# A bidirectional state-space layer with a feed-forward block: where zeroing, states, sums and one unit's restore are placed

## The chip, the cores and the metric

The kernel runs on one core of a Trainium2 chip. The metric is the time of one launch on the device in microseconds, as the median of some executions; lower is better. Engines: PE multiplies matrices, DVE, ACT and POOL work on vectors, SP only issues transfers. All of them run their own queues in order and wait for each other by semaphores.

## The reference

One layer (DEPTH = 1) over 1024 latent tokens of width 1024 with 256 context tokens ahead of them: a bidirectional S5 mixer (64 groups of 16 channels, 64 complex states each), a GLU, and a SwiGLU block of hidden width 2816. All in fp32.

```python
def run(u, h0):                                   # one direction
    bu = jnp.einsum('lgh,gnh->lgn', u.astype(F32), b_bar)
    bu = bu.at[0].add(lam_bar * h0)
    a = jnp.broadcast_to(lam_bar, bu.shape)
    _, h = lax.associative_scan(_linear_combine, (a, bu), axis=0)
    return jnp.einsum('lgn,ghn->lgh', h, c_mat).real, h[-1]
...
y = y.reshape(h.shape).astype(h.dtype) + d_skip * h      # forward + backward
g = jax.nn.gelu(y)
return g * jax.nn.sigmoid(g @ w_glu + b_glu)
...
x = x + m_l[2][:, None] * y_l
h_l = modulate(rms_norm(x, norm_ffn[i]), m_l[3][:, None], m_l[4][:, None])
x = x + m_l[5][:, None] * swiglu(h_l, ffn_w1[i], ffn_w3[i], ffn_w2[i])
```

## The kernel before

Tokens are cut into chunks of T = 8: 32 context chunks and 128 latent ones. Per chunk and group the inputs are summed into one state contribution, the states are scanned over the chunks, and an output is the sum of two parts: a Toeplitz product of the chunk's own inputs (`x_mm`) and a product of the state at its edge with coefficients CL (`states_mm` for half of the chunks, `states_all` for all). Groups come in eight units of 8 groups (0 to 7), two units to a quarter q. A unit's outputs are four groups of columns in two PSUM tiles, one for each parity of the group.

The scan runs on DVE (`scan`): 32 steps over two chunks each for the first 64 latent chunks, then 63 single steps. The odd chunks it skips in the first half are restored afterwards: for quarters 0 and 2 within the scan, for 1 and 3 by POOL (`fill`, op F). Early half means the states that the first 64 chunks of the scan give, late half the rest; backward states are turned into a buffer of their own (`turned`: R early, Z late, z both).

What runs beside the scan is written out by hand in the string PROG1, what runs after it in PROG2; `run` emits the operations in that order, and each engine's queue takes its instructions in the order of emission. A letter is an operation, its number a unit (K, P, R, N, D, H, Z, Q, z), twice a unit plus a parity (Y), a quarter and a part (C), or a load (T):

- C: `cl_ops`, one part of CL: two products on POOL and their sum, by PE and ACT (P in HOWS), POOL (E) or an accumulating DMA that POOL issues (Y).
- K: `k_mats`, the kernel matrices of half a quarter: 64-row products on PE into two PSUM tiles that ACT has zeroed before (`zeros`), two ACT copies, two writes to DRAM (`kd`) that ACT issues. T: SP loads them back as Toeplitz blocks KQ. T8 to T11 need K4 and K5, T12 to T15 need K6 and K7.
- P: early half of a unit, `x_mm` and then `states_mm`, which needs R; Y: two ACT copies of its tiles to SBUF. N: late half, D: two DVE adds of it onto Y.
- Q: a whole unit, `x_mm` and `states_all` (units 6 and 7). H: GELU on ACT. I, J: transposes for the GLU and their high and low parts. g: first GLU products.
- M, m, A, L, G, B: modulation, its loads, coefficient loads and signs.

The tiles of K, P and C come from a ring of three PSUM buffers (`pw`) beside two fixed ones, and those of PROG2 from eight (`pe8`) over the same eight banks. Later, in the FFN, each weight tile is split into a high part (ACT) and a low part, the rest (POOL): `op_split`, L1243. Its first four splits are emitted after the seventh GLU unit of the second half, L1261.

Of the kernel before, what the change touches and what calls it, by code (L numbers as in the profile page):

```python
# [17 lines left out]
P = 128  # L18
# [5 lines left out]
T = 8  # L24
G = 64
HC = 16
NS = 64
EPS = 1e-6
MAGIC = 12582912.0
HOWS = "PPPP PPEE PEEE EEEE"  # L30
ZEN = "VVSVSVSV"
PROG1 = ("A22 B0 A26 C02 G1 A30 A34 C03 A40 K0 A44 A48 C10 K1 L2 A54 G2 C11 A60 F10 C12 F11 C13 T0 T1 T2 T3 A64 M0 M1 K2 R0 P0 Y0 Y1 K3 L3 R1 C20 P1 Y2 Y3 T4 T5 G3 T6 T7 C21 C22 C23 K4 R2 P2 Y4 Y5 K5 R3 P3 Y6 Y7 T8 T9 T10 T11 C30 C31 R4 P4 Y8 Y9 C32 C33 R5 P5 Y10 Y11 K7 K6 M2 m0 F30 F31")
PROG2 = ("T12 T13 T14 T15 Z0 N0 Z1 Z2 D0 Z3 N1 D1 Z4 H0 H1 N2 D2 H2 w0 w1 l1 N3 Z5 D3 H3 N4 D4 z6 z7 I0 J0 I1 J1 H4 N5 D5 I2 J2 H5 I3 J3 W0 W1 W2 W3 x0 x1 x2 x3"
         " Q6 H6 I4 J4 Q7 I5 J5 V1 b0 w20 w21 l1 H7 g03 g13 I6 J6 g23 g05 g15 I7 J7 V2 g26 x10 x11 x12 x13")
LOG2E = 1.4426950408889634
LN2H = 0.693359375
LN2L = -2.12194440e-4
# [5 lines left out]
def s5_ffn_kernel(tc, a, out):  # L43
# [3 lines left out]
    with ctx:  # L47
# [16 lines left out]
        R0 = region("r0", 7)  # L64
# [594 lines left out]
        def cl_ops(q, part, ct, how):  # L659
# [7 lines left out]
            def add():  # L667
# [8 lines left out]
                else:  # L676
# [14 lines left out]
                 7: [(1, [0], 0, 8)], 8: [(1, [0], 8, 16)], 9: [(1, [1, 2, 3])],  # L691
                 11: [(2, [0], 0, 8)], 12: [(2, [0], 8, 16)], 13: [(2, [1, 2, 3])],
                 14: [(3, range(4), 0, 8)]}
        ct_ = [view(r, kb, [8, T, HC]) for r, kb in ((RW, 0), (RC[3], 0), (RC[3], 4), (RA, STB))]
        cts = [[ct_[0], ct_[0], ct_[1], ct_[2]], [ct_[0], ct_[1], ct_[2], ct_[0]], [ct_[1], ct_[2], ct_[0], ct_[1]], [ct_[3], ct_[0]] * 2]
        CL0 = cl_ops(0, 0, cts[0][0], SY) + cl_ops(0, 1, cts[0][1], SY)
        CLAT = {12: 1, 13: 1, 14: 2}
        for hb in range(16):
# [164 lines left out]
            while rest:  # L863
                one()

        def fill(q, h, reg, kb):

            tmps = [view(reg, kb + i, [256]) for i in range(2)]
            st, c0 = STQ[q], 32 * h
            for e in (0, 8):  # L870
                rot(st[:, 32 + c0:63 + c0:2, :, e:e + 8], st[:, 31 + c0:62 + c0:2, :, e:e + 8], LS[:, 0], 16 * q + e, E, tmps)

        MBd = dr.tile([2, 2, 512], F32, tag="mbd", name="mbd")

# [34 lines left out]
        def yview(k, gp):  # L909
            return Y[:, k].rearrange("p t (a e h) -> p e a t h", e=2, h=HC)[:, gp]  # L910

        def states_mm(k, pts, half, hs, start):

            for a_ in range(4):
                for ri in range(2):
                    for d in range(2):
                        cs_ = slice(64 * (half ^ d), 64 * (half ^ d) + 64)
                        c0 = 31 + 64 * half
                        for gp in range(2):
                            ps = slice(64 * gp, 64 * gp + 64)  # L920
                            st = hs[ps, :, ri, a_] if d else STQ[k // 2][ps, c0:c0 + 64, ri, 8 * (k % 2) + a_]
                            PE.matmul(flat(pts[gp][cs_, a_]), st, flat(CL[k // 2][ps, ri, d, 4 * (k % 2) + a_]),
                                      start=start and ri == 0, stop=ri == 1 and (start or a_ == 3))

        def states_all(k, pts, hs):

# [10 lines left out]

        def x_mm(k, pool):

            pts = [pool([4, T, HC]) for _ in range(2)]  # L940
            for a_ in range(4):
                for gp in range(2):
                    g = 2 * a_ + gp
                    kq = KQ[(2 * k + g // 4) % 4][:, g % 4].rearrange("p (t h) -> p t h", t=T)[:, ::-1]
                    PE.matmul(pts[gp][:, a_], U[:, 8 * k + g, 32:160], kq, start=a_ == 0, stop=False)
            return pts

        scan()
        inner = {}
        HSe = [view(r, kb, [64, 2, 4]) for r, kb in ((RC[3], 14), (RC[3], 12), (RC[3], 14), (RC[3], 12), (RA, 2), (RA, 0))]  # L950
        HSl = [view(RA, STB * (i // 3) + 4.125 + 2 * (i % 3), [64, 2, 4]) for i in range(6)]
        HSq = {6: view(RA, 0, [P, 2, 4]), 7: view(RA, STB, [P, 2, 4])}

        def run(prog):


            for w in prog.split():
                op, i = w[0], int(w[1:])
                if op == "A":
                    ada(i)  # L960
                elif op == "M":
                    mod_cols(i)
                elif op == "K":
                    k_mats(*divmod(i, 2), [zeros(pw([15 * HC])) if i == 6 else kt, zeros(pw([15 * HC])) if i in (0, 1, 2, 3, 6) else pm[:, 0:15 * HC]])
                elif op == "L":
                    cs_load(i, S)
                elif op == "G":
# [4 lines left out]
                elif op == "C":  # L972
                    q, part = divmod(i, 10)
                    for f in cl_ops(q, part, cts[q][part], HOW[q][part]):
                        f()
                elif op == "F":
                    fill(*divmod(i, 10), *((RW, 0) if i >= 30 else (RC[3], 12)))
                elif op == "T":
                    toeplitz(i)
                elif op == "R":  # L980
                    turned(i, 0, HSe[i], S)
                elif op == "Z":
                    turned(i, 1, HSl[i], ENG[ZEN[i]])
                elif op == "z":
                    turned(i, 2, HSq[i], ENG[ZEN[i]])
                elif op == "P":
                    inner[i] = x_mm(i, pw)
                    states_mm(i, inner[i], 0, HSe[i], False)
                elif op == "Q":
                    inner[i] = x_mm(i, pe8)  # L990
                    states_all(i, inner[i], HSq[i])
                elif op == "Y":
                    S.copy(yview(i // 2, i % 2), inner[i // 2][i % 2])
                elif op == "N":
                    late[i] = [pe8([4, T, HC]) for _ in range(2)]
                    states_mm(i, late[i], 1, HSl[i], True)
                elif op == "D":
                    for gp, po in enumerate(late[i]):
                        tt(yview(i, gp), po, yview(i, gp), ADD)
                elif op == "H":  # L1000
                    if i in late:
                        S.activation(Y[:, i], Y[:, i], AF.Gelu_apprx_tanh)
                    else:
                        for gp in range(2):
                            S.activation(yview(i, gp), inner[i][gp], AF.Gelu_apprx_tanh)
                elif op == "I":
                    if GH[0] is None:
                        GH[0] = tuple(view(region(t, 16, R32), 0, [4, 8, P]) for t in ("c1", "c0"))
                    late[i] = gt_hi(i, 0)
                elif op == "J":  # L1010
                    gt_lo(i, 0, late[i])
                elif op == "W":
                    if not W0:
                        W0.append(region("c2", 16, R32))
                        late["wh"] = view(W0[0], 0, [8, 512])
                    V.tensor_copy(view(W0[0], 4 * i, [1024]), wr0[i])
                elif op == "w":
                    cq, h = divmod(i, 10)
                    SY.dma_start(wr0[h], a["w_glu"][cq // 2][:, 1024 * h:1024 * h + 1024])
                elif op == "b":  # L1020
                    SY.dma_start(bglu, a["b_glu"].to_broadcast([P, D]))
                elif op == "l":
                    load_glu()
                elif op == "m":
                    mod_row(0)
                elif op == "x":
                    gate(i % 10, slice(4 * (i // 10), 4 * (i // 10) + 4))
                elif op == "V" and i == 2:
                    for j in range(4):
                        v = slice(1024 * j, 1024 * j + 1024)  # L1030
                        split(wr0[j], (WR[1][0][:, v], WR[1][1][:, v]), E)
                elif op == "V":
                    GR.append(region("ra", 80.5, R32))
                    GH[1] = (view(GR[0], 16, [4, 8, P]), view(GR[0], 32, [4, 8, P]))
                    WR.append((view(W0[0], 0, [8 * 512]), view(GR[0], 0, [8 * 512])))
                    WR.append((view(GR[0], 48, [8 * 512]), view(GR[0], 64, [8 * 512])))
                    for j in range(4):
                        v = slice(1024 * j, 1024 * j + 1024)
                        tt(WR[0][1][:, v], wr0[j], WR[0][0][:, v].bitcast(F32), SUB, (E, V)[j // 2])
                elif op == "g":  # L1040
                    glu_h(i // 10, i % 10 + 1)
# [198 lines left out]
            S.copy(o[0], x)  # L1240
            tt(o[1], x, o[0].bitcast(F32), SUB, eng)

        def op_split(ft, j, x):  # L1243
            o = ring[(4 * min(ft, NPL) + 7 * max(ft - NPL, 0) + j) % 4]
            OP_[ft, j] = o
            t_split([t.rearrange("p k n -> p (k n)") for t in o], x, E)

        RMS = {0: (0, 4), 4: (4, 6), 6: (6, 7)}
        for u in range(8):
# [8 lines left out]
            glu_unit(cq, s, *gens)  # L1258
            if u == 6:
                for j in range(4):  # L1260
                    op_split(0, j, raw[:, j])  # L1261
                raw13(1)
        together(rms_steps(7, 8))
        psE.__exit__(None, None, None)
# [520 lines left out]
```

## Time and profile before

| | us |
|---|---|
| median of three executions | 1013.72 (1013.44 to 1017.66) |
| profiled execution, whole | 1015.75 |
| profiled execution, span | 1014.0 |
| PE busy | 956.7 (94% of the span) |
| DVE, ACT, POOL busy | 781.7, 431.0, 761.1 |
| mean granted clock of PE | 0.991 |

The span runs from the first instruction to the last; the difference to the whole is what lies around it. Times in the rows below count from the span's start. Busy time of an engine doesn't say what bounds it: the tables of stretches and the waits do. The change lies between 195 and 260 us (end of PROG1, start of PROG2) and near 360 us (start of the FFN).

### The profile page before, as it was taken

Reading aid. Unit: us, or ns where it says so; the run is one execution under the profiler, and the core shown is the slowest. Engines: PE = TensorE matmul, PEld = TensorE weight load, DVE = VectorE, ACT = ScalarE, POOL = GpSimd, SP = SyncE. Lnnn points to the kernel's source line nnn. Section 1 sums busy time; section 2 is a strip of 40 time slices with the busy share of each in tenths; the row PEclk is TensorE's granted clock in tenths of the full one; section 3 lists DMA queues with packets and bytes.
Section 4 is the critical chain, followed back from the end, with each engine's and each line's share of the span. In section 5 each row is a group of like instructions: output and inputs, shape, how many; then the busy total and the mean of one; then the engine's idle time right before and its main releaser. Section 6 shows DMA issues by size and latency. Waiting matters only on the chain. (4 is left out here: it accounts for less than half of the span.)

```text
span 1014.0 us, 17677 instructions
## 1 busy us (share of the span) xinstructions
PE 956.7 (94%) x6604; PEld 751.5 (74%) x6604; DVE 781.7 (77%) x1594; ACT 431.0 (43%) x812; POOL 761.1 (75%) x590
## 2 busy tenths in 40 slices
PE   5988798879999999999999999999999999999996
PEld 1466523678888878778888888888888888888885
DVE  7979699996366767877959677686959677686887
ACT  5487622225444563443343343324343343324337
POOL 5799999994553448979785878777786877777764
PEclk9999999989999999999999999999999999999999
DMA  9765997325521021011212111121212111111205
GB/s 335 281 137 95 277 358 238 94 75 147 185 87 42 1 104 63 24 44 49 73 42 83 42 53 42 48 67 53 73 42 83 43 50 45 49 66 53 73 22 166
DMA packets 48542, 98.90 MB, mean 98 GB/s; under 512 B 4284, under 2 KB 18876, under 8 KB 47176
## 3 DMA queue, kind: packets, MB, share of 16 engines
q1 hardware_dynamic: 43272, 86.64, 25.8%
q0 software_dynamic: 2016, 7.34, 3.8%
q10 hardware_dynamic: 3168, 3.79, 1.1%
q8 instruction: 52, 0.85, 0.4%
q14 instruction: 34, 0.28, 0.1%
HBM read 84.25 MB, written 6.17 MB: 89 GB/s over the span
## 5 line engine op out<-in xcount | busy, mean ns | idle before, releaser
L77 POOL TENSOR_TENSOR c<-rxc,c 128x512 fp32r<-128x512 f32 x128 | 166.6, 1315 | 52.4 <-ACT c L1240 51.5
L1299 PE MATMUL ut<-ra,c 128*128 128x512 f32 x400 | 155.8, 389 | 1.2 <-DVE ra L77 1.2
L1298 PE MATMUL ut<-ra,c 128*128 128x512 f32 x400 | 155.8, 390 | 0.2 <-ACT ra L1240 0.2
L1300 PE MATMUL ut<-ra,c 128*128 128x512 f32 x400 | 155.7, 389 | 0.0
L1240 ACT CAST c<-rxc 128x512 fp32r<-128x512 f32 x128 | 79.0, 622 | 147.6 <-PE xt L1593 53.0
L1593 PE MATMUL xt<-c,c 128*128 128x512 f32 x540 | 129.7, 389 | 0.0
L1593 PEld LDWEIGHTS xt<-c,c 128*128 128x128 f32 x540 | 101.4, 188 | 21.0
L77 DVE TENSOR_TENSOR ru<-ru,xt 128x1024 f32<-128x1024 f32 x90 | 107.2, 1214 | 10.1 <-PE xt L1593 7.5
L77 DVE TENSOR_TENSOR ru<-ut,ru 128x512 f32<-128x512 f32 x98 | 67.1, 686 | 43.7 <-PE ut L1300 38.3
L1299 PEld LDWEIGHTS ut<-ra,c 128*128 128x128 f32 x400 | 75.1, 188 | 17.0 <-POOL rxc L77 1.5
L1298 PEld LDWEIGHTS ut<-ra,c 128*128 128x128 f32 x400 | 75.1, 188 | 16.1 <-ACT ra L1240 0.6
L1300 PEld LDWEIGHTS ut<-ra,c 128*128 128x128 f32 x400 | 75.1, 188 | 15.5
L77 POOL TENSOR_TENSOR c<-rw,c 128x512 fp32r<-128x512 f32 (+1 forms) x28 | 39.2, 1399 | 37.9 <-ACT c L1240 37.9
L77 POOL TENSOR_TENSOR c<-ru,c 128x512 fp32r<-128x512 f32 (+1 forms) x39 | 56.5, 1448 | 10.1 <-ACT c L1240 5.7
L1298 PE MATMUL ut<-c,c 128*128 128x512 f32 x160 | 62.4, 390 | 0.8 <-DVE rxa L77 0.8
L1300 PE MATMUL ut<-c,c 128*128 128x512 f32 x160 | 62.3, 389 | 0.0
L1299 PE MATMUL ut<-c,c 128*128 128x512 f32 x160 | 62.3, 389 | 0.0
L77 POOL TENSOR_TENSOR rxc<-rxc 128x512 f32<-128x512 f32 x40 | 60.6, 1514 | 1.6
L1593 PE MATMUL ut<-c,c 128*128 128x512 f32 x216 | 51.9, 389 | 0.0
L584 PE MATMUL pv<-ru,c 128*64 128x160 f32 x512 | 44.0, 314 | 7.3 <-POOL ru L77 2.6
L77 DVE TENSOR_TENSOR ru<-ru,ut 128x512 f32<-128x512 f32 x76 | 47.2, 678 | 0.3
L1593 PEld LDWEIGHTS ut<-c,c 128*128 128x128 f32 x216 | 40.6, 188 | 8.4
(446 smaller groups left out, 2397.7 us busy)
## 6 DMA issues: line engine op xcount, KB each, us to landing
c<-in_ada_w SPq DMA_DIRECT2D x46, 256.0 KB
rxc<-in_w SPq DMA_DIRECT2D x38, 256.0 KB
rxc<-in_w SPq DMA_DIRECT2D x19, 512.0 KB
ru<-in_w SPq DMA_DIRECT2D x11, 512.0 KB
rw<-in_w SPq DMA_DIRECT2D x11, 512.0 KB
ra<-in_ada_w SPq DMA_DIRECT2D x10, 512.0 KB
ra<-in_ada_w SPq DMA_DIRECT2D x18, 256.0 KB
ru<-in_xT SPq DMA_DIRECT2D x4, 1024.0 KB
```

The source lines that it names most:

```text
L77: eng.tensor_tensor(out=o, in0=x, in1=y, op=op)
L584: PE.matmul(pv[64 * (i % 2):64 * (i % 2) + 64, ri, c0:c0 + 160], w[:, i, 64 * ri:64 * ri + 64], U[:, 8 * b + 4 * j + i], start=True, stop= ...
L1240: S.copy(o[0], x)
L1298: PE.matmul(pu, wh, bh, start=start, stop=False)
L1299: PE.matmul(pu, wh, bl, start=False, stop=False)
L1300: PE.matmul(pu, wl, bh, start=False, stop=stop)
L1593: PE.matmul(pd, w[:, cs_], b, start=j in (1, 2, 4) and n == 0, stop=n == 2, skip_group_check=j not in (1, 2, 4))
```

## The change

- Unit 6 gets an early half of its own in PROG1 (R6, P6, Y12, Y13), without its Toeplitz product, which moves into its late half (N6), and its add D6. Q6 and z6 go; Z6 turns only the late half.
- The quarter-3 restore F30, F31 becomes F6 and F7, one unit each, with operations of twice the size.
- In P4 and P5 (and P6) the states come ahead of the Toeplitz product.
- O6 zeroes K6's two tiles before K7 is emitted.
- Three of the four sums of quarter 3 of CL go from POOL to accumulating DMAs, with one more buffer.
- The low part of the first FFN weight split goes from POOL to DVE.

```diff
-HOWS = "PPPP PPEE PEEE EEEE"
+HOWS = "PPPP PPEE PEEE YYYE"
-PROG1 = (" ... C30 C31 R4 P4 Y8 Y9 C32 C33 R5 P5 Y10 Y11 K7 K6 M2 m0 F30 F31")
+PROG1 = (" ... C30 C31 R4 P4 Y8 Y9 C32 C33 R5 P5 Y10 Y11 O6 K7 K6 M2 m0 F6 R6 P6 Y12 Y13 F7")
-PROG2 = ("T12 T13 T14 T15 Z0 N0 ... H2 w0 w1 l1 N3 Z5 D3 H3 N4 D4 z6 z7 I0 J0 ... x3"
-         " Q6 H6 I4 J4 Q7 I5 J5 ...")
+PROG2 = ("T12 T13 T14 T15 Z0 N0 ... H2 w0 w1 l1 Z6 N3 Z5 D3 H3 N4 D4 z7 I0 J0 ... x3"
+         " N6 D6 H6 I4 J4 Q7 I5 J5 ...")
-        ct_ = [view(r, kb, [8, T, HC]) for r, kb in ((RW, 0), (RC[3], 0), (RC[3], 4), (RA, STB))]
-        cts = [ ... , [ct_[3], ct_[0]] * 2]
+        ct_ = [view(r, kb, [8, T, HC]) for r, kb in ((RW, 0), (RC[3], 0), (RC[3], 4), (RA, STB), (RA, STB + 4.125))]
+        cts = [ ... , [ct_[3], ct_[0], ct_[4], ct_[3]]]
+        def fill_k(k):
+            tmps = [view(RW, 2 * i, [512]) for i in range(2)]
+            st, e = STQ[k // 2], 8 * (k % 2)
+            rot(st[:, 32:95:2, :, e:e + 8], st[:, 31:94:2, :, e:e + 8], LS[:, 0], 8 * k, E, tmps)
...
-                                      start=start and ri == 0, stop=ri == 1 and (start or a_ == 3))
+                                      start=start and a_ + ri == 0, stop=stop and ri == 1 and a_ == 3)
...
-            pts = [pool([4, T, HC]) for _ in range(2)]
+            new = not isinstance(pool, list)
+            pts = [pool([4, T, HC]) for _ in range(2)] if new else pool
...
+                elif op == "O":
+                    KO[i] = [zeros(pw([15 * HC])) for _ in range(2)]
...
-                    k_mats(*divmod(i, 2), [zeros(pw([15 * HC])) if i == 6 else kt, zeros(pw([15 * HC])) if i in (0, 1, 2, 3, 6) else pm[:, 0:15 * HC]])
+                    k_mats(*divmod(i, 2), KO.get(i) or [kt, zeros(pw([15 * HC])) if i < 4 else pm[:, 0:15 * HC]])
...
                 elif op == "P":
-                    inner[i] = x_mm(i, pw)
-                    states_mm(i, inner[i], 0, HSe[i], False)
+                    if i > 3:
+                        inner[i] = [pw([4, T, HC]) for _ in range(2)]
+                        states_mm(i, inner[i], 0, HSe[i], True, i == 6)
+                        if i < 6:
+                            x_mm(i, inner[i])
+                    else:
+                        inner[i] = x_mm(i, pw)
+                        states_mm(i, inner[i], 0, HSe[i], False)
...
                 elif op == "N":
-                    late[i] = [pe8([4, T, HC]) for _ in range(2)]
-                    states_mm(i, late[i], 1, HSl[i], True)
+                    late[i] = [pe8([4, T, HC]) for _ in range(2)] if i < 6 else x_mm(i, pe8)
+                    states_mm(i, late[i], 1, HSl[i], i < 6)
...
-        def op_split(ft, j, x):
+        def op_split(ft, j, x, eng=E):
...
-                    op_split(0, j, raw[:, j])
+                    op_split(0, j, raw[:, j], E if j else V)
```

## Rows read from the trace of the kernel before

**Rows 1.** Stretches of 20 us: length, busy us of each engine, granted clock, DMA.
```profile
200.00:220.00 20.00, 15.29 (x365) 14.21 (x368) 18.68 (x77) 4.00 (x8) 19.77 (x10) 0.84 0.25 68
...
260.00:280.00 20.00, 20.00 (x105) 16.57 (x101) 8.43 (x7) 9.10 (x12) 14.43 (x6) 1.00 0.62 211
```
**Rows 2.** PE's waits from 125 to 275 us: total, times, longest.
```profile
PE pw L809 <- ACT pw L771: 4.1, 4, 2.0
```
**Rows 3.** Timeline, SP and PE, Toeplitz loads and x products: start, length, idle before.
```profile
207.70 4.79 SPq L830 DMA_DIRECT2D ra<-kd  x4
...
213.03 1.13 PE L945 MATMUL pw<-ra,ru 128*128 128x128 f32 x8 [3.79 <-DMA ra<-kd]
215.07 2.07 PE L945 MATMUL pw<-ra,ru 128*128 128x128 f32 x8 [0.92 <-DMA ra<-kd]
```
**Rows 4.** Stretches of PE: P4, P5 states; K7, K6; Q6's x product, states.
```profile
217.07:220.78 3.71, 3.71 (x64) 0.50 0.17 63
223.22:225.50 2.28, 2.27 (x64) 1.00 0.00 0
...
225.43:227.11 1.68, 1.68 (x146) 1.00 0.04 10
229.15:231.11 1.96, 1.96 (x145) 1.00 0.22 71
...
246.98:249.38 2.40, 2.10 (x16) 1.00 0.68 280
...
249.31:253.58 4.27, 4.26 (x128) 1.00 0.02 4
```
**Rows 5.** Timeline of POOL: a DMA sum's issue, the last add, the last restore.
```profile
130.52 0.88 POOL L675 DMA_DIRECT2D c<-rw  x1 [0.30 <-POOL rw L77]
...
219.15 2.36 POOL L77 TENSOR_TENSOR c<-c,rw 128x1024 f32<-128x1024 f32 x1
...
232.48 1.53 POOL L77 TENSOR_TENSOR ra<-ra,rw 128x256 f32<-128x256 f32 x2
```
**Rows 6.** Timeline of ACT: Y6 and Y7, K6's first copy, a turned copy.
```profile
209.28 1.07 ACT L993 COPY ru<-pw 128x512 f32<-128x512 f32 x2 [2.34 <-PE pw L922]
...
231.21 0.36 ACT L821 COPY r<-pw 128x240 f32<-128x240 f32 x1 [1.82 <-issue]
...
232.72 0.62 ACT L902 COPY ra<-ra 128x512 f32<-128x512 f32 x1 [0.40 <-ACT r L821]
```
**Rows 7.** DMA queues at 55:60, 120:122, 124:126, 209:213: packets, MB, share.
```profile
q0 software_dynamic: 144, 0.52, 55.5%
...
q1 hardware_dynamic: 358, 0.65, 98.3%
...
q1 hardware_dynamic: 91, 0.17, 25.2%
...
q1 hardware_dynamic: 1030, 0.52, 54.8%
```
**Rows 8.** All state products (L922): one wait of PE's, us and times.
```profile
  ACT r L821: 0.3, 1
```
**Rows 9.** Timeline of DVE: the first turned copies behind the scan.
```profile
227.77 1.29 DVE L904 COPY ra<-ra 128x512 f32<-128x512 f32 x2
```
**Rows 10.** Timeline of PE: N0, the first FFN products, the last transposes.
```profile
233.39 1.88 PE L922 MATMUL pe<-c,ra 64*64 64x128 f32 x52 [0.57 <-issue]
...
362.23 0.51 PE L1300 MATMUL pu<-c,c 128*128 128x512 f32 x1 [1.32 <-POOL c L77]
...
370.09 1.04 PE L1193 MATMUL pd<-r,rxa 128*128 128x128 f32 x8
...
374.31 0.50 PE L1299 MATMUL pu<-ra,c 128*128 128x512 f32 x1 [0.23 <-POOL ra L77]
```
**Rows 11.** Timeline of DVE near 366 and 387 us.
```profile
366.13 1.06 DVE L77 TENSOR_TENSOR r<-r 128x1 f32<-128x1 f32 x1
...
386.74 1.05 DVE L77 TENSOR_TENSOR c<-ru,c 128x512 fp32r<-128x512 f32 x1 [0.69 <-ACT c L1309]
```

More of the change, by code (lines that the diff above doesn't have):

```diff
@@ L29 @@
 MAGIC = 12582912.0
-HOWS = "PPPP PPEE PEEE EEEE"
+HOWS = "PPPP PPEE PEEE YYYE"
 ZEN = "VVSVSVSV"
-PROG1 = ("A22 B0 A26 C02 G1 A30 A34 C03 A40 K0 A44 A48 C10 K1 L2 A54 G2 C11 A60 F10 C12 F11 C13 T0 T1 T2 T3 A64 M0 M1 K2 R0 P0 Y0 Y1 K3 L3 R1 C20 P1 Y2 Y3 T4 T5 G3 T6 T7 C21 C22 C23 K4 R2 P2 Y4 Y5 K5 R3 P3 Y6 Y7 T8 T9 T10 T11 C30 C31 R4 P4 Y8 Y9 C32 C33 R5 P5 Y10 Y11 K7 K6 M2 m0 F30 F31")
-PROG2 = ("T12 T13 T14 T15 Z0 N0 Z1 Z2 D0 Z3 N1 D1 Z4 H0 H1 N2 D2 H2 w0 w1 l1 N3 Z5 D3 H3 N4 D4 z6 z7 I0 J0 I1 J1 H4 N5 D5 I2 J2 H5 I3 J3 W0 W1 W2 W3 x0 x1 x2 x3"
-         " Q6 H6 I4 J4 Q7 I5 J5 V1 b0 w20 w21 l1 H7 g03 g13 I6 J6 g23 g05 g15 I7 J7 V2 g26 x10 x11 x12 x13")
+PROG1 = ("A22 B0 A26 C02 G1 A30 A34 C03 A40 K0 A44 A48 C10 K1 L2 A54 G2 C11 A60 F10 C12 F11 C13 T0 T1 T2 T3 A64 M0 M1 K2 R0 P0 Y0 Y1 K3 L3 R1 C20 P1 Y2 Y3 T4 T5 G3 T6 T7 C21 C22 C23 K4 R2 P2 Y4 Y5 K5 R3 P3 Y6 Y7 T8 T9 T10 T11 C30 C31 R4 P4 Y8 Y9 C32 C33 R5 P5 Y10 Y11 O6 K7 K6 M2 m0 F6 R6 P6 Y12 Y13 F7")
+PROG2 = ("T12 T13 T14 T15 Z0 N0 Z1 Z2 D0 Z3 N1 D1 Z4 H0 H1 N2 D2 H2 w0 w1 l1 Z6 N3 Z5 D3 H3 N4 D4 z7 I0 J0 I1 J1 H4 N5 D5 I2 J2 H5 I3 J3 W0 W1 W2 W3 x0 x1 x2 x3"
+         " N6 D6 H6 I4 J4 Q7 I5 J5 V1 b0 w20 w21 l1 H7 g03 g13 I6 J6 g23 g05 g15 I7 J7 V2 g26 x10 x11 x12 x13")
 LOG2E = 1.4426950408889634
@@ L693, in s5_ffn_kernel @@
                  14: [(3, range(4), 0, 8)]}
-        ct_ = [view(r, kb, [8, T, HC]) for r, kb in ((RW, 0), (RC[3], 0), (RC[3], 4), (RA, STB))]
-        cts = [[ct_[0], ct_[0], ct_[1], ct_[2]], [ct_[0], ct_[1], ct_[2], ct_[0]], [ct_[1], ct_[2], ct_[0], ct_[1]], [ct_[3], ct_[0]] * 2]
+        ct_ = [view(r, kb, [8, T, HC]) for r, kb in ((RW, 0), (RC[3], 0), (RC[3], 4), (RA, STB), (RA, STB + 4.125))]
+        cts = [[ct_[0], ct_[0], ct_[1], ct_[2]], [ct_[0], ct_[1], ct_[2], ct_[0]], [ct_[1], ct_[2], ct_[0], ct_[1]], [ct_[3], ct_[0], ct_[4], ct_[3]]]
         CL0 = cl_ops(0, 0, cts[0][0], SY) + cl_ops(0, 1, cts[0][1], SY)
@@ L864, in scan, with fill_q @@
                 one()
-        def fill(q, h, reg, kb):
-            tmps = [view(reg, kb + i, [256]) for i in range(2)]
+        def fill_q(q, h):
+            tmps = [view(RC[3], 12 + i, [256]) for i in range(2)]
             st, c0 = STQ[q], 32 * h
@@ L910, in yview, with states_mm @@
             return Y[:, k].rearrange("p t (a e h) -> p e a t h", e=2, h=HC)[:, gp]
-        def states_mm(k, pts, half, hs, start):
+        def states_mm(k, pts, half, hs, start, stop=True):
             for a_ in range(4):
@@ L944, in x_mm @@
                     kq = KQ[(2 * k + g // 4) % 4][:, g % 4].rearrange("p (t h) -> p t h", t=T)[:, ::-1]
-                    PE.matmul(pts[gp][:, a_], U[:, 8 * k + g, 32:160], kq, start=a_ == 0, stop=False)
+                    PE.matmul(pts[gp][:, a_], U[:, 8 * k + g, 32:160], kq, start=new and a_ == 0, stop=not new and a_ == 3)
             return pts
         scan()
[L949 to L952, printed above, removed]
+        inner, KO = {}, {}
+        HSe = [view(r, kb, [64, 2, 4]) for r, kb in ((RC[3], 14), (RC[3], 12), (RC[3], 14), (RC[3], 12), (RA, 2), (RA, 0), (RA, 2))]
+        HSl = [view(RA, STB * (i // 4) + 4 + 2 * (i % 4), [64, 2, 4]) for i in range(7)]
+        HSq = {7: view(RA, STB, [P, 2, 4])}
         def run(prog):
@@ L976, in run @@
                 elif op == "F":
-                    fill(*divmod(i, 10), *((RW, 0) if i >= 30 else (RC[3], 12)))
+                    if i < 10:
+                        fill_k(i)
+                    else:
+                        fill_q(*divmod(i, 10))
                 elif op == "T":
@@ L986, in run @@
                 elif op == "P":
-                    inner[i] = x_mm(i, pw)
-                    states_mm(i, inner[i], 0, HSe[i], False)
+                    if i > 3:
[3 more added lines that the diff above has]
+                            x_mm(i, inner[i])
+                    else:
+                        inner[i] = x_mm(i, pw)
+                        states_mm(i, inner[i], 0, HSe[i], False)
                 elif op == "Q":
@@ L1241, in t_split @@
             tt(o[1], x, o[0].bitcast(F32), SUB, eng)
-        def op_split(ft, j, x):
+        def op_split(ft, j, x, eng=E):
             o = ring[(4 * min(ft, NPL) + 7 * max(ft - NPL, 0) + j) % 4]
             OP_[ft, j] = o
-            t_split([t.rearrange("p k n -> p (k n)") for t in o], x, E)
+            t_split([t.rearrange("p k n -> p (k n)") for t in o], x, eng)
         RMS = {0: (0, 4), 4: (4, 6), 6: (6, 7)}
```

## The prediction

> **What bounds the kernel now.** I read the 20 us table first [rows 1]. From 200 to 220 us PE is busy for 15.29 of 20 us while POOL has hardly a free moment; from 260 to 280 PE is busy in every microsecond. So a microsecond taken from PE's queue, or from what it waits for, ahead of 260 moves the end by as much; work taken off POOL counts only where PE waits for POOL. Then the waits: PE's wait for ACT in front of kernel-matrix products is 4.1 us in four waits, the longest 2.0 [rows 2]; that one stands between the products K7 and K6, where one ends at 227.11 and the other starts at 229.15 [rows 4]. The larger wait is the timeline's [rows 3]: SP issues the four Toeplitz loads T8 to T11 from 207.70, and PE stands 3.79 us until T8 lands and 0.92 more until T9 lands, at 215.07. Unit 4's states then run for 3.71 us at a granted clock of 0.50 (1.2 GHz), where unit 5's take 2.28 at 1.00 (2.4 GHz) [rows 4]. From 215.07 PE is one chain: x product of unit 4, its states, the same for unit 5, K7, the wait, K6, N0. N0's second tile waits for ACT's first copy of K6's result, which ends at 231.57 (231.21 plus 0.36) [rows 6, 8]. So this stretch takes 231.57 - 215.07 = 16.5 us. The scan on DVE is out of the way by 227.8 [rows 9].
>
> **Part by part.** (1) *States ahead of the Toeplitz product, units 4 and 5.* Unit 4's 64 matmuls now run while T8 and T9 are on their way: they need only R4, which ACT has copied by about 211 (its copies of unit 3 start at 209.28 and take 1.07, R4 takes 0.62) [rows 6]. For unit 5 the order costs: its states now wait for Y8, Y9 and R5 on ACT, 1.07 + 0.62 us and about 0.1 of hand-over, which before lay beside the x product.
>
> (2) *Zeroing ahead (O6).* ACT's two zeroings, behind Y11, now lie beside K7's 1.68 us. The 2.04 us in front of K6 goes. If that cover were gone, it would be back, no more.
>
> (3) *Unit 6's early half in the scan (P6).* It puts on PE's queue, between K6 and N0, 64 matmuls of 2.28 us, and in front of them a wait: R6 stands on ACT behind K6's two copies and two DMA issues, and starts 232.72 - 231.11 = 1.61 us after K6's end [rows 4, 6]; it takes 0.62. N0 and everything behind it queue there. Behind P6 come Y12 and Y13, 1.07 us: the two tiles of P6 take the buffers that follow K6's, and N0's second tile already waited for one of those [rows 8], so N0 waits for Y13.
>
> The new stretch, from T9's landing to N0's second tile: half an x product 1.13 [rows 3], Y8 and Y9 1.07, R5 0.62, hand-over 0.1, states 2.28, x 2.10, K7 1.68, K6 1.96, drain 1.61, R6 0.62, P6 2.28, Y12 and Y13 1.07: **16.5 us, as before**. What parts 1 and 2 take out, part 3 puts back. It gets it back later: unit 6 is left with 64 state matmuls where states_all had 128, 4.27 - 2.28 = **2.0 us off PE** inside the stretch that PE bounds [rows 4]. Its adds D6 (two of about 0.7 us) go on DVE and its GELU on ACT behind them; PE has the whole of Q7 (4.27 us and an x product) before it needs them, so nothing.
>
> (4) *Three sums by DMA.* An add holds POOL for 2.36 us; issuing a DMA sum takes 0.88, and 0.30 of waiting for the product in front of it [rows 5]. Three times 2.36 - 1.18 is 3.5 us off POOL. The last add would end near 218.0 instead of 221.51, and K7 comes at 222.4 by the sum of part 3, so on PE's chain this is worth **0**. The restores, on POOL from the last add to 234.01 in 12.5 us [rows 5], become F6, half of them and done near 224.3, and F7. R6 can start at 227.7 by the same sum, so F6 has 3.4 us in hand; without them R6 and P6 would slip by what is missing.
>
> The price is on the DMA engines. One sum keeps all 16 busy for 55.5% of 5 us, 2.78 us [rows 7]. By POOL's order they are issued near 200, 205 and 210 (my estimate, back from the last add). The second meets the writes of K5's matrices, for which SP's T8 waits until 207.70, and the third meets T8 and T9. When a sum runs, the plain loads beside it fall from 358 packets in 2 us to 91 [rows 7]. So T9 lands later by something between 0 and two whole sums, 5.6 us. The loads use the engines at 54.8% [rows 7], so half a sum can fit beside them, and K5's writes are nearly over when the second sum's first packets appear: I take half of one sum, **+1.4 us**, and keep both ends.
>
> The Trainium skill (DMA: Bandwidth & Descriptors, "Queues, rings and completion order") says that each DMA engine takes turns between its queues a packet at a time, whatever the sizes, so small packets wait behind large ones. By that rule the toll is nearer the upper end, the rival below. The two windows just named agree with it in direction.
>
> (5) *One low part by VectorE.* PE stands 1.32 us before the third matmul of the FFN for POOL's first low part [rows 10]. DVE, free at that moment, can have it earlier; such an operation took 1.05 us beside POOL [rows 11]. But 8 us on come the transposes of the last unit (370.09) and at 374.31 a wait for POOL behind them: they hang on DVE's row statistics, not on PE, so an earlier PE only waits there, unless that chain gets shorter too. It may: one of its tiny operations took 1.06 us while POOL had a low part running [rows 11], and POOL now ends one operation (1.3 us) sooner. So between 0 and -1.3; I take **-0.7**.
>
> The Trainium skill (SBUF — State Buffer, "Who interferes with whom") has a VectorE operation with two SBUF inputs wait out a GpSimd operation that reads SBUF. The 1.06 us row agrees; by that rule the new low part itself waits for POOL, and the gain would be 0.3 rather than 0.7.
>
> **The sum**: 0 - 2.0 + 1.4 - 0.7 = -1.3 us against the profiled execution (span 1014.0, 1015.75 with what lies around it), so a span near 1012.7. That execution is 2.0 us above the median of the three shown, 1013.72; off the median the forecast is 1012.4.
>
> **Rivals.** *The sums hold up the Toeplitz loads (slower).* Mechanism: K5's writes and T8, T9 each lie under a whole sum, and PE, idle as long as in rows 3, runs unit 5 at the lower clock as it ran unit 4. Price: 5.6 for 1.4, and 3.71 - 2.28 = 1.4 more: 1012.4 + 4.2 + 1.4 = 1018.0. It decides once T9 lands more than 2.7 us later than in rows 3, which eats parts 3 and 5 whole. For it: the fall to 91 packets. Against: the loads leave 45% of the engines free. Chance 0.25.
> *Everything fits (faster).* T9 lands as before, N0's tiles lie in other buffers (-1.07), the stall of 0.57 in N0 that no wait explains [rows 10] doesn't come back, part 5 gives its 1.3: -2.0 - 1.07 - 0.57 - 1.3 = -4.9, 1008.8. Between that and the forecast lies most of this case. Chance 0.2.
> *The states don't fill the wait*, because R4 or a tile comes late: they run behind T9, +2.28, 1014.7. Chance 0.05.
> The forecast, within 1.5 us of 1012.4, has 0.5.
>
> **Numbers.** Range 1009.3 to 1017.8: the lower end leaves out the last of the fast case, the upper the worst of the contention. Half a per cent, about what a measurement of this kernel can tell from no change, is 5.1 us: below 1008.65 or above 1018.8. Faster 0.08, same 0.87, slower 0.05.
>
> **What would show it.** In the changed profile: no wait for ACT before K6; unit 4's states ahead of its x product at full clock; R6 right behind K6's second DMA issue, and PE idle some 2 us before P6; 64 state matmuls where 128 stood near 250; the landing of T9, against 215.07 (this is the term I know least); the wait of 1.32 us at 361 gone and a wait near 369 or 373 in its place. I am wrong if T9 lands more than 3 us late, if N0 starts well ahead of Y13, or if PE shows new gaps between 232 and 345.

## The result

The changed kernel is slower. Its median is 1019.68 us (1016.16 to 1026.32); the kernel before, on the same chip, has 1015.61 us (1012.01 to 1017.81). The ratio is 1.0042, 95% interval [1.0026, 1.0057], which is +4.3 us of 1015.6 (interval +2.6 to +5.8).

The profiled execution of the changed kernel took 1022.03 us, span 1020.2, so it is 2.4 us above its median, while that of before lay at its own (1015.75). Between the two traces stand 6.2 us, a little more than between the kernels. Of the changed kernel's 17 executions 8 lie at 1016.2 to 1017.9 us, 6 at 1022.0 to 1026.3 and 3 between; the traced one is among the six, so its trace shows the dear case.

The views of the changed kernel, in the order in which those of before were read. First the transfers: the timeline of ACT, POOL and SP, with start, length, and in brackets the idle time before and what ended it. They answer to [rows 3] and the DMA issue of [rows 5].

```profile
206.43 0.33 ACTq L822 DMA_DIRECT2D kd<-rw  x1
207.19 0.79 ACTq L822 DMA_DIRECT2D kd<-rw  x1
...
206.29 0.87 POOL L675 DMA_DIRECT2D c<-rw  x1 [0.30 <-POOL rw L77]
210.89 2.02 POOL L77 TENSOR_TENSOR ra<-rxc,rxa 128x1024 f32<-128x1024 f32 x1 [1.66 <-PE pw L928]
213.20 0.87 POOL L675 DMA_DIRECT2D c<-ra  x1 [0.30 <-POOL ra L77]
...
211.49 4.12 SPq L830 DMA_DIRECT2D ra<-kd  x4
```

The second sum goes out 0.90 us ahead of the second write of K5's matrices. SP issues T8 once that write has landed: at 211.49, 4.3 us behind the write's issue. In the kernel before it was 207.70, 1.75 us behind the write (timeline of ACT):

```profile
205.95 0.33 ACTq L822 DMA_DIRECT2D kd<-rw  x1
```

So T8 goes out 3.8 us later, and only 2.55 of it is the longer time of the write. The other 1.24 is the write's own later issue, which comes without a sum as well: in c, a kernel below without any of the DMA sums, the write goes out at 207.06. The DMA queues over that stretch (207.2 to 211.45; packets, MB, share of 16 engines), and those of the kernel before over the stretch that answers to it (205.9 to 207.7):

```profile
q0 software_dynamic: 144, 0.52, 65.1%
q10 hardware_dynamic: 288, 0.25, 18.5%
```

```profile
q10 hardware_dynamic: 288, 0.25, 41.1%
```

The same 288 packets of K5's writes (q10) stand alone before, in 1.8 us; now they share 4.25 us with a whole sum (q0), which takes more than three times as much of the engines.

PE, timeline of the changed kernel from P4's states to the first product of the FFN that waited [rows 3, 4, 10]:

```profile
212.61 2.25 PE L928 MATMUL pw<-c,ra 64*64 64x128 f32 x60 [0.52 <-ACT ra L908]
216.32 1.16 PE L952 MATMUL pw<-ra,ru 128*128 128x128 f32 x8 [1.46 <-DMA ra<-kd]
218.83 2.08 PE L952 MATMUL pw<-ra,ru 128*128 128x128 f32 x8 [1.35 <-DMA ra<-kd]
...
231.98 0.46 PE L809 MATMUL pw<-c,rxa 64*16 64x112 f32 x18 [1.80 <-issue]
235.65 3.70 PE L928 MATMUL pw<-c,ra 64*64 64x128 f32 x60 [1.32 <-ACT ra L908]
...
240.50 7.09 PE L928 MATMUL pe<-c,ra 64*64 64x128 f32 x219 [0.94 <-ACT ru L1011]
...
368.35 0.50 PE L1318 MATMUL pu<-c,c 128*128 128x512 f32 x1 [0.64 <-DVE c L77]
```

Unit 4's states do lie in the wait for T8, at full clock. But the wait behind them isn't used up: 1.46 us for T8 and 1.35 for T9, which landed only at 218.8 instead of 215.07. There is no wait for ACT's zeroing in front of K6 any more; instead PE stands 1.80 us inside K6, with nothing in the trace to end it ("issue"). Unit 6's states (235.65) wait for R6, and N0's second tile (240.50) for Y13, as foreseen. The same stretches with their granted clock (length, busy us, clock, DMA share, GB/s): x product's second half, P5's states, P6's states (the last with N0's first two products):

```profile
218.83:220.90 2.07, 2.07 (x9) 0.50 0.64 125
222.16:225.78 3.62, 3.62 (x61) 0.53 0.52 150
235.65:239.56 3.91, 3.91 (x62) 0.54 0.26 73
```

In the kernel before only one run of states, P4's, was at 0.50 [rows 4]; now P4's are at full clock, and P5's and the new P6's at 0.53 and 0.54.

### The profile page after: what moved, and what is told of

It is laid out like the page before. It is cut to its first block, busy times and chain, and to the rows that moved or that the text cites. A ratio compares the mean times of both kernels' runs of the same rounds, so it can differ in the third digit from the quotient of the medians.

```text
span 1020.2 us, 17681 instructions
## 1 busy us (share of the span) xinstructions
PE 960.1 (94%) x6604; PEld 754.1 (74%) x6604; DVE 783.6 (77%) x1597; ACT 432.5 (42%) x814; POOL 753.7 (74%) x581
## 5 line engine op out<-in xcount | busy, mean ns | idle before, releaser
L77 POOL TENSOR_TENSOR ru<-ru,rxa 128x512 f32<-128x512 f32 (+1 forms) x13 | 22.4, 1758 | 41.3 <-PE pe L1077 41.3
L77 POOL TENSOR_TENSOR c<-rxc,rxa 128x1024 f32<-128x1024 f32 x23 | 47.7, 2145 | 0.1
```

The source lines that it names most:

```text
L77: eng.tensor_tensor(out=o, in0=x, in1=y, op=op)
```

## The experiments

All times in the table are ratios to the kernel before on the same chip, and what that is of 1015.6 us.

| kernel | what it holds | ratio [95%] | us |
|---|---|---|---|
| changed | everything | 1.0042 [1.0026, 1.0057] | +4.3 |
| b | states first | 0.9967 [0.9951, 0.9984] | -3.4 |
| c | zeroing ahead | 0.9998 [0.9979, 1.0017] | -0.2 |
| e | unit 6's early half | 1.0028 [1.0014, 1.0042] | +2.8 |
| f | three sums by DMA | 1.0015 [0.999, 1.0039] | +1.5 |
| g | states first, low part | 0.997 [0.9955, 0.9986] | -3.0 |
| i | states first, low part, zeroing | 0.9965 [0.9951, 0.9978] | -3.6 |
| m | states first, low part, first sum | 0.9967 [0.995, 0.9984] | -3.4 |
| j | everything but unit 6 | 0.9995 [0.9976, 1.0013] | -0.5 |
| a | everything, no sum by DMA | 1.0012 [0.9995, 1.003] | +1.2 |
| h | everything, first sum alone | 0.9995 [0.9978, 1.0011] | -0.5 |
| k | everything, first and second sum | 1.0026 [1.0009, 1.0043] | +2.6 |
| l | everything, first and third sum | 0.9999 [0.9978, 1.0021] | -0.1 |
| n | h, restore and R6 ahead of K7 | 1.0007 [0.9992, 1.0022] | +0.7 |

### One part alone

**b, states ahead in units 4 and 5.**

```diff
                 elif op == "P":
-                    inner[i] = x_mm(i, pw)
-                    states_mm(i, inner[i], 0, HSe[i], False)
+                    if i > 3:
+                        inner[i] = [pw([4, T, HC]) for _ in range(2)]
+                        states_mm(i, inner[i], 0, HSe[i], True, False)
+                        x_mm(i, inner[i])
+                    else:
+                        inner[i] = x_mm(i, pw)
+                        states_mm(i, inner[i], 0, HSe[i], False)
```

> The kernel before with the states of units 4 and 5 ahead of their Toeplitz products as the only edit. By part 1: K7 starts 7.2 us after T9's landing instead of 10.4, so 3.2 us faster, 1.4 of it because unit 4's states no longer run at the lower clock. Rival (the clock falls all the same, now under unit 5's states, and these also wait for R5): 0.5 to 1.5 us faster.

Measured -3.4 us, as the theory had it. Stretches of PE in b, the states of P4 and P5 with their clock:

```profile
211.06:213.31 2.25, 2.25 (x61) 1.00 0.60 140
216.88:219.14 2.26, 2.26 (x61) 1.00 0.04 7
```

Both run at full clock; before, P4's took 3.71 us at 0.50, behind the load [rows 4].

**c, zeroing ahead.**

```diff
-... R5 P5 Y10 Y11 K7 K6 M2 m0 F30 F31
+... R5 P5 Y10 Y11 O6 K7 K6 M2 m0 F30 F31
```

> The kernel before with K6's two tiles zeroed ahead of K7 as the only edit. By the prediction's part 2: the wait of 2.04 us in front of K6 goes, 2.0 us faster. Rival (in the changed kernel PE stands 1.80 us inside K6 with no wait to show for it, so the time that the zeroing took was also the time in which something else caught up): the gap moves from ahead of K6 to inside K6, and the time falls by 0 to 0.5 us.

Measured -0.2 us, and not -2.0 (the interval ends at -2.1). Timelines of PE in c, and in i (states, low part and zeroing), inside K6:

```profile
230.19 0.46 PE L809 MATMUL pw<-c,rxa 64*16 64x112 f32 x18 [1.31 <-issue]
```

```profile
227.04 0.46 PE L809 MATMUL pw<-c,rxa 64*16 64x112 f32 x18 [2.10 <-issue]
```

> The kernel before with states ahead in units 4 and 5, zeroing ahead (O6) and VectorE's first low part; sums and unit 6 as before. Theory (an issue stall takes the place of the wait for zeroing): PE's wait of 2.04 us in front of K6 is gone, a gap without a releaser of 1.3 to 1.9 us stands inside K6 instead, and the time is 0 to 0.7 us under the same kernel without the zeroing, ratio about 0.9965. Rival: where the states have been moved the stretch runs through, no such gap is seen, and it is 2 us under it, ratio 0.995 or less.

Kernel i differs from g by `O6` alone (`K7 K6` to `O6 K7 K6`) and is 0.6 us faster, within the intervals. In c, i and all other kernels here that have O6 (changed, a, h, j, k, l, n) the gap stands in front of the same 18 products of K6, with 1.3 to 2.1 us. In the kernel before, where PE waits 2.04 us for ACT just ahead of K6, nothing stops it inside. So the wait was a cover: in the kernels that keep the wait (before, b, e, f, g, m) the gap is absent, and in those without it PE stands 1.3 to 2.1 us. What PE lacks there the traces do not name. The trace has a transfer of 16 KB on the queue it names "instruction" in these stretches, which would fit code that comes late. But the kernel before has such a transfer too, near 227.0, as its wait for ACT begins; late code is an inference, and no experiment here separates it.

**e, unit 6's early half alone.**

```diff
-... Y10 Y11 K7 K6 M2 m0 F30 F31
+... Y10 Y11 K7 K6 M2 m0 F6 R6 P6 Y12 Y13 F7
-T12 ... l1 N3 Z5 D3 H3 N4 D4 z6 z7 ... Q6 H6 ...
+T12 ... l1 Z6 N3 Z5 D3 H3 N4 D4 z7 ... N6 D6 H6 ...
```

> The kernel before, with unit 6's early half alone moved into the scan's program (F6, R6, P6, Y12, Y13, F7; N6 and D6 for Q6); units 4 and 5, zeroing, sums and low part as before. Theory: PE's queue pays for it in full, because P6 stands between K6 and N0 with waits on both sides: drain 1.61 + R6 0.62 + states 2.28 + Y12 and Y13 1.07, less the stall of 0.57 that stood in N0 = +5.0 us at N0's second tile, and -2.0 us back where unit 6 has 64 state products instead of 128. So +3.0 us against the kernel before, ratio 1.003; N0's second tile near 236.5 where it was 231.57. Rival: part of it lies in time in which PE would have stood anyway, and the total is within 1 us of the kernel before (0.999 to 1.001). A second rival: POOL, which has all its sums to do, brings the restore late, and it is over 4.5 us slower.

Measured +2.8, as the theory had it. PE's stretch of P6's states in e, and its timeline at K6 and at N0:

```profile
232.50:236.24 3.74, 3.74 (x62) 0.57 0.29 72
```

```profile
227.99 1.44 PE L809 MATMUL pw<-c,rxa 64*16 64x112 f32 x59 [2.04 <-ACT pw L771]
...
237.19 10.21 PE L928 MATMUL pe<-c,ra 64*64 64x128 f32 x318 [0.94 <-ACT ru L1004]
```

N0's second tile stands at 237.19, 5.6 us later than before; 2.0 come back later. The theory had 236.5: the largest thing it missed is the clock, 0.57, by which the new states took 3.5 us behind their wait (60 products, which took 2.25 in b). R6 was ready 2.2 us behind K6, as reckoned; PE ran P6's first four products in that time and then stood 1.09. Against the clock stands that K6 had ended 0.87 us earlier in this trace than in that of before (230.24 to 231.11).

**f, three sums by DMA alone.**

```diff
-HOWS = "PPPP PPEE PEEE EEEE"
+HOWS = "PPPP PPEE PEEE YYYE"
```

> The kernel before with the three sums of quarter 3 by DMA as the only edit. Contention: 3 to 5 us slower than before, T9 2.5 us later after K5's second write is issued. Rival (unit 6): within 1 us of the kernel before, since POOL's queue is not on PE's chain and the loads share the engines.

Measured +1.5 us with an interval from -1.0 to +4.0: neither the 3 to 5 of the theory nor the 1 of the rival, and it alone decides little. Its timeline, ACT, POOL and SP:

```profile
206.80 1.01 ACTq L822 DMA_DIRECT2D kd<-rw  x1
...
207.39 0.88 POOL L675 DMA_DIRECT2D c<-rw  x1 [0.30 <-POOL rw L77]
...
209.27 4.78 SPq L830 DMA_DIRECT2D ra<-kd  x4
```

Here the sum goes out 0.59 us behind the write, and T8 follows 2.5 us after the write; T9 landed at 216.88, 10.1 us behind the write where it was 9.1 before.

**g and m, low part and first sum on top of b.** In g VectorE takes the first low part (`op_split(0, j, raw[:, j], E if j else V)`); m adds `HOWS = "PPPP PPEE PEEE YEEE"`.

> The kernel before, with the states of units 4 and 5 ahead of their Toeplitz products and with VectorE's first low part; nothing else. Theory: the two gains add, -3.3 and -0.7 = -4.0 us, ratio 0.996; PE's gap before the third matmul of the FFN is near 0.65 where it was 1.32. Rival: the gain of the low part is hidden behind the transposes of the last unit, and it is no more than states ahead alone, -3.3 us, with a gap of 1.0 to 1.3 later on.

> The kernel before with states ahead in units 4 and 5, VectorE's first low part and the first of the three sums by DMA; no zeroing ahead, unit 6 as before. Theory: POOL is done with its last add before K7 needs it, so PE's wait of 0.28 us for POOL in front of K7 goes and nothing else changes: 0 to 0.5 us under the same kernel without that sum, ratio 0.9965 against the kernel before. Rival: the sum delays K4's or K5's writes and it is 1 us or more over it, ratio 0.998 or more.

Timeline of PE in g, before the third product of the FFN:

```profile
361.38 0.50 PE L1306 MATMUL pu<-c,c 128*128 128x512 f32 x1 [0.64 <-DVE c L77]
```

The gap is halved, 1.32 to 0.64 us [rows 10], but g isn't faster than b, and m isn't than g: 0.7 us is less than these intervals show. Both, like b and i, beat the kernel before and the changed one; of the versions made here these four are the best, and they can't be told apart. The low part has no run of its own; the 0.7 used for it below is what its gap shrank by.

### The changed kernel with one part less

**a, all sums on POOL** (`HOWS` of before).

> The changed kernel with the three sums of quarter 3 back on POOL; all else as changed. Theory of contention (the second DMA sum holds up the write of K5's matrices, the write holds up T8 to T11, and the longer idle time of PE brings the lower clock): 4.5 to 6 us off the changed kernel, so between 2 us below and 0.5 us above the kernel before; K5's second write lands 1.7 us after its issue (4.2 in the changed kernel), T9 lands within 1 us of 215. Rival (unit 6's early half, put between K6 and N0, is what costs): it stays within 1.5 us of the changed kernel, 3 to 4 us above the kernel before.

Measured +1.2, 3.1 below the changed kernel: between the theory (4.5 to 6 below) and the rival (within 1.5). K5's writes and T9 are on time and P5's states at full clock. But POOL is now in the chain, as PE's timeline in front of K7, of P6 and of its second part shows:

```profile
222.76 0.27 PE L809 MATMUL kt<-c,rxa 64*16 64x112 f32 x1 [1.09 <-POOL c L77]
...
228.33 0.49 PE L928 MATMUL pw<-c,ra 64*64 64x128 f32 x4 [0.58 <-POOL ra L77]
...
229.99 3.45 PE L928 MATMUL pw<-c,ra 64*64 64x128 f32 x60 [1.17 <-ACT ra L908]
```

**h, k and l: which sum it is.** The changed kernel with `YEEE`, `YYEE` and `YEYE` as the last word of `HOWS`.

> The changed kernel with only the first of the three sums as a DMA; the other two go back to POOL. Theory: it is the second sum, running over the writes of K5's matrices, that makes T8 to T11 late and drops the clock, so without it K5's second write lands 1.7 to 2.0 us after its issue, T9 lands by 215.5, unit 5's states run at full clock, and the total is 2.5 to 3 us below the changed kernel, ratio to the kernel before 1.001 to 1.002. Rival: the sums are not the cause, the time is within 1 us of the changed kernel (ratio 1.003 to 1.005).

> The changed kernel with the first and the second sum as DMAs, the third back on POOL. With the first sum alone it was 0.5 us under the kernel before, with all three 4.2 us over it; the question is which of the two does that. Theory: the second, which runs over K5's writes, for which T8 to T11 wait. Then K5's second write takes about 4 us from issue to landing, T9 lands 2 to 4 us after 215, PE stands in front of unit 4's x products, and the time is 3 to 4.5 us over the kernel before (ratio 1.003 to 1.0045). Rival: the third, which runs beside T8 to T11 themselves; then this kernel is within 1 us of the kernel before, and PE doesn't stand there.

> The changed kernel with the first and the third sum as DMAs, the second back on POOL. Theory (the second sum is the cause): K5's writes land within 2 us of their issue, T8 to T11 are issued as early as in the kernel before, and the third sum beside them costs at most 1 us, since they want little more than half of the DMA engines: ratio 0.999 to 1.0005. Rival (the third is the cause, or half of it): T9 to T11 land 2 us late and unit 5's x product stands for them, ratio 1.002 or more.

The first sum by itself removes what POOL cost in a: h is 1.7 us under a and 1.5 to 2.5 under what was expected of it, though the intervals of a and h overlap. All three cost 4.8 us more than the first alone; the second brings 3.1 of it (k against h), the third, without the second, 0.4 (l against h), within the error. The interval of such a difference is about 2.5 us to either side. Timelines of h and of k, K5's second write on ACT, the second sum on POOL (k), T8 to T11 on SP:

```profile
206.98 0.44 ACTq L822 DMA_DIRECT2D kd<-rw  x1
...
208.85 4.03 SPq L830 DMA_DIRECT2D ra<-kd  x4
```

```profile
204.97 0.77 ACTq L822 DMA_DIRECT2D kd<-rw  x1
...
205.42 0.86 POOL L675 DMA_DIRECT2D c<-rw  x1 [0.30 <-POOL rw L77]
...
207.18 5.17 SPq L830 DMA_DIRECT2D ra<-kd  x4
...
215.25 1.16 PE L952 MATMUL pw<-ra,ru 128*128 128x128 f32 x8 [1.03 <-DMA ra<-kd]
```

The theory has the size of k nearly right (+2.6 for 3 to 4.5) and its place wrong in this execution: the sum went out 0.45 us behind the write, the write took 2.2 us, and PE stood only 0.40 + 1.03 us for the loads. In l the write took 2.1 us to T8's issue, T8 and T9 came in time, and unit 5's x product stood 1.24 us for T11, beside the third sum. The rest of what k's trace has over h's lies later, in N0 and N1. The same 219 and 100 products in k and in h:

```profile
235.11:243.65 8.54, 8.54 (x219) 0.78 0.88 252
245.56:250.42 4.86, 4.86 (x100) 0.65 0.04 15
```

```profile
234.08:241.17 7.09, 7.08 (x219) 1.00 0.87 236
242.09:245.57 3.48, 3.48 (x100) 1.00 0.55 224
```

That is 2.8 us of lower clock, and between the two stretches PE stands 1.91 us in k and 0.92 in h. No wait ties this to the sum. So that the second sum costs about 3 us is measured; that all of it goes through K5's writes is not.

**j, everything but unit 6.** `PROG1`, `PROG2` and the restores as before, with O6.

> The changed kernel without unit 6's early half: states ahead in units 4 and 5, zeroing ahead, three sums by DMA, VectorE's low part; unit 6 and its restore as before. Theory, by adding what the parts alone measured: -3.3 (states), 0 (zeroing), -0.7 (low part), +1.5 (sums) = -2.5 us, ratio 0.9975; the changed kernel stands 6.7 us above it, which is the price of unit 6's early half there. If the sums cost more where states fill PE's wait, the 3 us that stood between the changed kernel and the one with its sums on POOL: -1.0 us, ratio 0.999. Rival: unit 6 costs little, and this kernel is within 2 us of the changed one, ratio 1.002 or more.

Measured -0.5; the changed kernel stands 4.8 us above it, e 2.8 above the kernel before. So unit 6's early half costs 3 to 5 us; whether it costs more in company, the intervals don't tell. Against the sum of the parts (-3.4 - 0.2 - 0.7 + 1.5 = -2.8) j has lost 2.3, which the intervals just allow as error. Its trace shows the plainest case of sums over loads (ACT, POOL, SP, then PE), but it was taken in an execution of 1020.07 us, 4.5 above j's median, so it is not what j pays each time:

```profile
206.48 0.33 ACTq L822 DMA_DIRECT2D kd<-rw  x1
...
205.92 0.87 POOL L675 DMA_DIRECT2D c<-rw  x1 [0.30 <-POOL rw L77]
212.05 0.87 POOL L675 DMA_DIRECT2D c<-ra  x1 [0.30 <-POOL ra L77]
...
211.84 7.00 SPq L830 DMA_DIRECT2D ra<-kd  x4
...
217.02 1.16 PE L946 MATMUL pw<-ra,ru 128*128 128x128 f32 x8 [3.30 <-DMA ra<-kd]
221.99 2.08 PE L946 MATMUL pw<-ra,ru 128*128 128x128 f32 x8 [3.81 <-DMA ra<-kd]
```

The second sum goes out 0.56 us ahead of the write, and T8 follows 5.4 us behind the write; the third goes out 0.2 us behind T8, and T9 lands 10.1 us behind T8's issue, where it took 7.4 [rows 3].

**From the second write of K5's matrices to T8's issue**, over the kernels: no second sum: 1.75 to 2.1 (before, h and all others); sum 0.45 and 0.59 us behind the write: 2.2 (k), 2.5 (f); sum 0.56 and 0.90 us ahead of it: 5.4 (j), 4.3 (changed). In these four traces, one execution each, the order in which two engines issue within a microsecond goes with 2 to 3 us. The time of that write itself lies between 204.97 and 207.19 in the traces, so the order, and the toll with it, need not be the same each time. Whether that is what spreads the changed kernel's times is not shown: there is one trace of each kernel.

**n, restore and R6 ahead.** From h:

```diff
-... Y10 Y11 O6 K7 K6 M2 m0 F6 R6 P6 Y12 Y13 F7
+... Y10 Y11 O6 F6 R6 K7 K6 M2 m0 P6 Y12 Y13 F7
```

> The changed kernel with only the first sum by DMA, and with F6 and R6 emitted ahead of K7, so that R6 doesn't stand behind K6's copies and writes on ACT. Theory (the wait for R6 and the lower clock behind it are the better part of unit 6's price): PE's wait of 1.29 us in front of unit 6's states is gone, they run at full clock in 2.3 us where they took 3.7, and the time is 2 to 3 us under the same kernel without this move, ratio to the kernel before 0.9965 to 0.998. Rival: the clock falls at the next gap instead (in front of N0), only the wait of 1.3 us comes back or nothing at all: 0 to 1.3 us under it, ratio 0.998 to 0.9995. Second rival: R6 waits on ACT for POOL's restore with K7's copies queued behind it, and it is slower.

Measured 1.2 us over h, within the error: the second rival, or no difference. Timelines of ACT and of PE in n:

```profile
226.48 0.62 ACT L908 COPY ra<-ra 128x512 f32<-128x512 f32 x1 [3.50 <-POOL ra L77]
...
228.92 0.36 ACT L821 COPY r<-pw 128x240 f32<-128x240 f32 x1 [0.75 <-ACT rw L821]
```

R6 now waits 3.50 us for POOL's restore, K7's copies queue behind it and K6's behind those, and P6's second tile lies in a buffer that K6's copy frees: PE stood 1.66 us for that copy, where it stood 1.29 for R6. P6's products behind it took 3.70 us at a clock of 0.50. The wait has another name and the price is the same.

## Why the prediction was wrong

It said no change, 1012.4 us (-1.3); measured was +4.3. Its slower rival, sums that hold up the loads with a lower clock behind them, stood at 1018.0, +4.3 over the median it reckoned from. Three steps of the forecast failed: the 2.04 us in front of K6 counted as gained (c measured 0.2), unit 6's early half costed at full clock, and the sums' toll taken as 1.4. The slower rival's own condition, T9 more than 2.7 us late, came true (3.8, of it 2.55 by the write under the sum), and so did the forecast's first sign of being wrong, T9 more than 3 us late. That the rival also had the number is partly luck: the sums made T9 late by far less than its two whole sums, the zeroing gave nothing back, and the lower clock cost more than its 1.4.

**The stretch of PE, step by step.** N0's second tile stood at 231.57 and now at 240.50, 8.9 us later, where the forecast had 1.4. T9's second half of the x product starts 3.8 us later (215.07 to 218.83), and from there to N0 it is 21.7 us where the forecast had 16.5. The terms of those 16.5 as they came: half an x product 2.07 for 1.13 (clock 0.50), Y8 to R5 1.26 for 1.79 (they began under the product), P5's states 3.62 for 2.28 (clock 0.53), K6 with its gap 3.82 for 1.96, drain 1.79 for 1.61, P6's states behind their wait to Y13 4.85 for 3.35 (clock 0.54), the rest within 0.2. Of these 5.2 us, 3.8 are the lower clock and 1.9 the issue gap, less some 0.5 that ran side by side.

**Part 1, states ahead: right.** The wait was filled as described; alone it is worth 3.4 us (b). The forecast used it to pay for part 3.

**Part 2, zeroing ahead: a wait counted as gain.** "The 2.04 us in front of K6 goes" is true of the wait, not of the time. An issue gap of 1.3 to 2.1 us takes its place (c, i, changed). The forecast named what hides ACT's zeroings; it did not ask what the wait itself hid. The kernel before had a stall of that kind in N0, 0.57 us [rows 10], and the forecast took it for something that might go, not for something that might grow.

**Part 3, unit 6: the way right, the clock not.** P6 waited for R6, N0 for Y13, and 64 state matmuls stand where 128 stood: of the 8.9 us at N0, 6.1 are left at the third product of the FFN (362.23 to 368.35), 2.0 of the 2.8 between for unit 6, whose 64 products took 2.27 us (forecast 2.0), and 0.7 for the low part (forecast 0.7). But all of it was costed at full clock. In all seven kernels that have unit 6's early half (changed, a, e, h, k, l, n) its states took 3.45 to 3.70 us behind their wait and not 2.28. The lower clock comes behind the gaps that PE has in or ahead of K6 and in front of P6. Alone the part costs 2.8 us (e). The forecast's even account, parts 1 and 2 paying for part 3, came out -3.4 - 0.2 + 2.8 = -0.8 by parts instead of -2.0, 1.2 us short. With the sums (+1.5) and the low part (-0.7) the parts alone add up to 0.0, and the whole measured +4.3. That difference is about what the intervals of these runs allow together (some 4 us), so how much more the parts cost in company is not shown.

**Part 4, the sums: the term that was mis-sized.** The taken value was +1.4, with 5.6 as the far end. The second and third together cost 4.8 us in the changed kernel against h. The estimate of the sum's issue, 205, was right to 1.3 us (206.29), but "K5's writes are nearly over when the second sum's first packets appear" was not: the second write was issued 0.90 us behind the sum, and T8, which waits for it, went out after 4.3 us instead of 1.75: a toll of 2.55 in this trace. Nor was half a sum the right toll: the 288 packets of the writes took as long as the whole sum beside them. Here the rule from the Trainium skill (DMA: Bandwidth & Descriptors, "Queues, rings and completion order"), that a DMA engine takes turns between its queues and drains a whole packet before it switches, pointed the right way, to more than 1.4. The traces of j (5.4 us) and of the changed kernel (4.3) agree in direction; those of k (2.2) and f (2.5), where the sum was issued second, show next to no toll. A thing the forecast missed altogether: the new buffer of the third sum lies on states that P3 still reads, so POOL waited 1.66 us for PE (210.89). But the third sum, issued at 213.20, did T9 no harm here: T9 landed 7.3 us behind T8's issue, as before (7.4), where in j it took 10.1 and in l PE stood 1.24 us for T11.

**Part 4, POOL: a part of it is worth something.** The forecast put the 3.5 us off POOL at 0 on PE's chain. In a, PE waits 1.09 + 0.58 us for POOL, and one sum by DMA takes that away. The slack was real only as long as PE came late to K7, and part 1 brought it there earlier: in g PE waits 0.28 us for POOL in front of K7, in i 0.58.

**Part 5, low part: right in the trace** (1.32 to 0.64 us), below what times of whole kernels can show.

**Range.** The upper end, 1017.8, is 4.1 us over the 1013.72 that the forecast reckoned from, and the measured +4.3 lies at that edge; the kernel before itself has 1015.61 over 17 executions, 1.9 us more than the three that the forecast had. The lower clock, the issue gap and a whole sum over the writes are three prices, and the upper end had two of them, for P5's states and the sum. A chance of 0.05 for more than half a per cent was little for a change that puts three transfers of 512 KB onto the stretch in which PE waits for loads, though +2.6 to +5.8 leaves open whether that came true.

## What to carry to other kernels

A wait that is taken away may have hidden another; before it is counted as gain, look for stalls without a releaser nearby, and test the one edit alone: here the states put first, one small edit, held the whole gain (-3.4 us) and the rest of the change lost it. A large transfer that is moved to an idle-looking queue is to be placed against the small transfers on which loads depend, by the order of issue to a microsecond, and if that order can't be held, by the dear case. Work that is inserted behind a gap of PE is costed at the lower clock if the gaps of that stretch have brought it on before; here that was 1.2 to 1.5 us for the states of one unit.

## What the runs showed of the hardware

- A write of 120 KB in small packets (288 for two such writes) let the load that waits for it go 1.75 to 2.1 us after its issue when alone, and 4.3 and 5.4 us after it with an accumulating DMA of 512 KB (144 packets) issued 0.90 and 0.56 us ahead of it (changed, j). With the same sum issued 0.45 and 0.59 us behind the write it was 2.2 and 2.5 us (k, f).
- PE stands without a releaser at a fixed place of its program, in front of the last 18 products of one group (45 stand ahead of them), 1.3 to 2.1 us in nine kernels, unless it has waited for another engine just ahead of the group (2.04 us, 2.38 in f): then not at all, in six.
- The granted clock was 0.50 to 0.58 (1.2 GHz for most of the stretch) for unit 6's states, which came behind gaps of 1.1 to 2.1 us that lay a few us apart, and 1.00 for the states of units 4 and 5 in b, where gaps of 0.5 to 0.7 us stood ahead of them. The length of a gap doesn't tell: PE stood 2.04 us in front of K6 in b, and no lower clock followed, but in e, g and m the same wait was followed by 0.50 from 230 to 232. Behind waits of 1.00 and 0.52 us P5's states ran at 0.54 in m; behind 0.40, 1.03 and 0.52 they ran at 1.00 in k.
